# Seven quarter products in the MLP's up projection: one pair of units at a time

## The chip, the cores and the metric

The kernel runs on one core of one Trainium2 chip. The metric is the device time of one execution in microseconds. Five engines work from their own instruction streams: TensorE (PE, matmuls), VectorE (DVE), ScalarE (ACT), GpSimd (POOL) and SyncE (SP, which issues nearly all DMAs here). Matmul results go to PSUM, eight banks of 512 float32 values per partition. Everything else lies in SBUF.

## The reference, cut to what matters

Two layers of a hybrid decoder block for one sequence of 512 tokens with model width 1024, all in float32. Each layer has two mixing branches (a gated delta rule and a sliding-window attention), merged and projected, and then an MLP, which is what the change touches:

```python
h2 = rmsnorm(x, pre_mlp_g)                              # (512, 1024)
ff = jnp.square(jax.nn.relu(h2 @ w_ff1)) @ w_ff2        # 1024 -> 4096 -> 1024
x = x + rmsnorm(ff, post_mlp_g)
```

## The kernel before, in words

**Precision.** A float32 product is made of three matmuls of the rounded type float32r. Each operand is split into a high part (an ACT cast) and a low part (a DVE subtraction), and hi·hi, hi·lo and lo·hi are added in PSUM. So every weight chunk costs a load (SP), a cast `wh` (ACT, L323) and a subtraction `wl` (DVE, L324), all in `prefetch`.

**Weights.** `specs` lists all chunks in the order in which they are used. A chunk is 128 x 1024 values. `weights()` hands out the next one and calls `prefetch`, which prepares chunks up to three ahead of it: `LOOK` = 4 buffers each of `wh` and `wl`, and `WR` = 5 raw buffers `wr` that the loads fill. A `wh` buffer is free again after the last matmul that reads it.

**The MLP.** The 4096 hidden columns are four blocks s = 0 to 3 of 1024. A block has eight *units* of 128 hidden columns. One unit of the up product `h2 @ w_ff1` is `mm_a`: one weight chunk, eight slices of the contraction, three matmuls each, 512 tokens wide, into one bank of the pool "pm" (two banks). ACT then takes relu and square.

In blocks 0 to 2 the down product is done by a Strassen-Winograd scheme with seven products P1 to P7 instead of eight. `lefts` (L1345 on) makes the sums and splits of the activations for four units at once, `seven` makes the sums of weight quarters on DVE (`add`, L293), and `mm_c` (L400 to L404) multiplies: two chunks of 12 matmuls per product. The products stand in the order P1, P5, P6, P4, P7, P2, P3 and are added into `acc` by DVE. Block 3 is plain: eight units, then `mm_b4` for the first 512 output columns and `mm_b` or `last_tiles` for the others.

**Banks.** The tags are "pm" (2 banks, `PM`), "ps" (3, `PS`), "pk" (1, `PK`) and "ss" (2, `PZ`).

**Order.** A scheduler decides the order of instructions on each engine when the program is built, from priorities and its own estimate of times; on the chip each engine then runs its list in that fixed order. Where the source opens an `Order`, the instructions of the named engines keep the order of the source. A new tile takes a slot of its tag that has been released, and waits for one if there is none. `X4` is a tag of six 128 x 1024 tiles that raw activations, gains and residual rows share; `T[i]` are tags of four 128 x 512 tiles.

Of the kernel before, what the change touches and what calls it, by code (L numbers as in the profile page):

```python
# [49 lines left out]
PMB = 2  # L50


def chunk_order(depth):


    out = []
    for l in range(depth):
        a_in = lambda w, c: out.append(("chunk", w, l, 0, c, 0))
        b_in = lambda w, r, c, n: out.append(("chunk", w, l, r, c, n))
        for n in range(3):  # L60
            for j in range(4):
                b_in("w_in", j * 256, OFF_B + n * NB, NB)
        n_ = {"K": 0, "G": 0, "A": 0}
        for c in "".join(MIX):
            a_in("w_in", {"K": OFF_K, "G": OFF_GB, "A": OFF_GA}[c] + n_[c] * P)
            n_[c] += 1
        for h in range(H):
            for o in (OFF_V, OFF_Q, OFF_Z):
                a_in("w_in", o + h * P)
            if h == 0:  # L70
                for m in range(KT):
                    a_in("w_up_sw", m * P)
                for m in range(NA, NA2):
                    a_in("w_in", OFF_GA + m * P)
        for m in range(NA2, KT):
            a_in("w_in", OFF_GA + m * P)
        for m in range(KT):
            a_in("w_up_dn", m * P)
        for n in range(2):
            for j in range(4):  # L80
                b_in("w_o", j * 256, n * 512, 512)
        for s in range(4):
            for m in FF_ORDER if s < 3 else range(8):
                a_in("w_ff1", (s * 8 + m) * P)
            if s < 3:
# [34 lines left out]
def hybrid_trunk(ctx, tc, x, positions, pre_mix_g, dn_conv_w, dn_a_log, dn_dt_bias, dn_norm_g,  # L120
# [26 lines left out]
        return sm.tile([P, n], F32, name=name, bufs=1)  # L147

    US = pool_of("s", 8)
    T = [pool_of(f"t{i}", 4) for i in range(8)]  # L150

    def UQ(name, dt=F32):

# [37 lines left out]
    def c4(ap):  # L191
        return ap.rearrange("p (c i) -> p c i", c=4)
# [77 lines left out]
    def load(key):  # L270
# [3 lines left out]
        dma(wr[:, :w], wpk[index[key], :, :w])  # L274
        return wr

    def blocks(a, n_):
        return a[:, :2 * n_ if n_ else 1024].rearrange("p (k c) -> p k c", k=2 if n_ else 8)

    def seven(w, l, r0):  # L280

# [10 lines left out]
        def add(i, k, j):  # L292
# [22 lines left out]
    def prefetch(n, wr=None, sub=tt):  # L315
        while len(pre) < min(n, len(specs)):
# [5 lines left out]
            w = 2 * n_ if n_ else 1024  # L322
            nc.scalar.copy(wh[:, :w], wr[:, :w])  # L323
            sub(out=wl[:, :w], in0=wr[:, :w], in1=wh[:, :w].bitcast(F32), op=ALU.subtract)  # L324
            pre.append((blocks(wh, n_), blocks(wl, n_)))
# [65 lines left out]
    def mm_c(pss, left, onto=False):  # L391

        for j in range(2):
            wh, wl = weights()
            hi, lo = left[j]
            for t in range(2):
                for r in range(2):
# [6 lines left out]
                    mm(pss[t], lhsT=lo[:, c], rhs=wh[:, r, :], start=False, stop=last,  # L404
                       skip_group_check=onto)
# [34 lines left out]
    def root(xt):  # L440
        return rstd("nr", meansq(xt[:, :512], "nq0"), meansq(xt[:, 512:], "nq1"))

    def norm_half(xt, gb, r, g):

        xs = T[7]("xs")
# [21 lines left out]
        for g in range(2):  # L467
            turned(pss[g], t, qs[g])

    def post_tiles(tiles, a0g, ps1, add1, q0, gb, xsrc, xdst, gb2=None):  # L470


        n = range(len(tiles))
        rows = [slice(t * P, (t + 1) * P) for t in tiles]
        xt = [[T[5 + i]("xt") for i in range(2)] for t in tiles]
        for i in n:
            for k in range(2):
                dma(xt[i][k], xsrc[rows[i], k * 512:(k + 1) * 512])
# [19 lines left out]
        if gb2 is not None:  # L498
            q = [(meansq(xo[i][:, :512], "nq0"), meansq(xo[i][:, 512:], "nq1")) for i in n]
            for i in n:  # L500
                r = rstd("nr", *q[i])
                xs.append([norm_half(xo[i], gb2, r, g) for g in range(2)])
        order.end()
        return xs

# [14 lines left out]
    for l in range(depth):  # L520
# [816 lines left out]

        def ff2_tail(tiles, pss):
            a0, a1 = [a[0] for a in acc], [a[1] for a in acc]
            if l == depth - 1:  # L1340
                post_tiles(tiles, a0, pss, a1, s0, gb3, xd, give)
            else:
                xs_next.extend(post_tiles(tiles, a0, pss, a1, s0, gb3, xd, keep, nxt[0]))

        def lefts(X, Y):  # L1345

            a11, a21, a12, a22 = X[:, 0:512], X[:, 512:1024], Y[:, 0:512], Y[:, 512:1024]
            S = {n_: T[4](n_) for n_ in ("S1", "S2", "S3", "S4")}
            tt(out=S["S1"], in0=a21, in1=a22, op=ALU.subtract)
            tt(out=S["S2"], in0=a11, in1=S["S1"], op=ALU.subtract)  # L1350
            for name, U, src in (("P1", T[5], a11), ("P5", T[7], S["S1"]), ("P6", T[1], S["S2"]),
                                 ("P4", T[2], a22), ("P7", T[3], S["S3"]), ("P2", T[6], a12),
                                 ("P3", T[0], S["S4"])):
                if name == "P4":
                    tt(out=S["S4"], in0=a12, in1=S["S2"], op=ALU.subtract)
                    tt(out=S["S3"], in0=a21, in1=a11, op=ALU.subtract)
                p_ = pair(U, name)
                split(src, *p_)
                left[name].append(p_)

        for s in range(3):
            left = {f"P{i}": [] for i in range(1, 8)}
            raw = [None, None]
            for i, m in enumerate(FF_ORDER):
                if s == 0 and i < 4:
                    ps = early[i][0]
                else:
                    ps = PM("ps_f1")
                    mm_a(ps, h2)

                if i % 4 < 2:
                    raw[i % 2] = X4("raw")
                r_ = raw[i % 2].rearrange("p (a k n) -> p a k n", a=2, k=2)[:, :, m % 2, :]
                act(out=r_, in_=ps.rearrange("p (a n) -> p a n", a=2), func=AF.Relu)
                act(out=r_, in_=r_, func=AF.Square)
                if i % 4 == 3:
# [3 lines left out]
            v_ = [T[4]("p1") for t in range(2)]  # L1380
            for t in range(2):
                nc.scalar.copy(v_[t], pa[t])
            mm_c(pb_, left["P5"])
            for t in range(2):
                into(2 + t, 1, pb_[t])
            pc = [PS("ps_p6"), PK("ps_p6")]
            mm_c(pc, left["P6"])
            for t in range(2):
                tt(out=v_[t], in0=pc[t], in1=v_[t], op=ALU.subtract)
# [1 line left out]
                    nc.scalar.copy(acc[t][1], v_[t])  # L1391
                else:
                    tt(out=acc[t][1], in0=acc[t][1], in1=v_[t], op=ALU.add)
            pc = [PM("ps_p4"), PM("ps_p4")]
            mm_c(pc, left["P4"])
            for t in range(2):
                into(2 + t, 0, pc[t])
            pc = [PS("ps_p7"), PK("ps_p7")]
            mm_c(pc, left["P7"])
            for t in range(2):  # L1400
                tt(out=v_[t], in0=pc[t], in1=v_[t], op=ALU.add)
                for n, op in ((0, ALU.subtract), (1, ALU.add)):
                    tt(out=acc[2 + t][n], in0=acc[2 + t][n], in1=v_[t], op=op)
            mm_c(pa, left["P2"], True)
            for t in range(2):
                into(t, 0, pa[t])
            mm_c(pb_, left["P3"], True)
            for t in range(2):
                tt(out=acc[t][1], in0=pb_[t], in1=acc[t][1], op=ALU.add)


        gb3 = gain(post_mlp_g[l])
        h3 = []
        for m in range(8):
            ps = PM("ps_f1")
            mm_a(ps, h2)
            r_ = T[4]("relu")
            act(out=r_, in_=ps, func=AF.Relu)
            act(out=r_, in_=r_, func=AF.Square)
            p_ = pair(T[m % 4], "h3")  # L1420
            split(r_, *p_)
            h3.append(p_)
        pss = four(1)
        mm_b4(pss, h3)
        for t in range(NT):
# [40 lines left out]
```

## Time and profile before

| | |
|---|---|
| Median of three runs | 1830.43 us (1829.82 to 1830.57) |
| Span of the profiled execution | 1828.6 us |
| Time of the profiled execution itself | not listed; the median lies 1.8 us above its span |
| PE busy | 1809.1 us (99%) |
| Weight loads (PEld) busy | 1503.9 us (82%) |
| DVE busy | 1292.1 us (71%) |
| ACT busy | 940.9 us (51%) |
| POOL busy | 211.2 us (12%) |
| HBM read | 239.38 MB |

PE's busy time counts each matmul from its start to a modelled end, and consecutive matmuls overlap. So the rate is read from the distance between starts. Busy shares are averages over the whole span; the MLP's stages are read from a view that cuts the span into stretches. Rows of a group give its line, engine, operation, output and inputs, shapes and count, then busy time, mean length, and the engine's idle time before them with what ended it.

### The profile page before, as it was taken

What the parts mean: (1) busy time and instruction counts of PE and PEld (TensorE: products, weight loads), DVE (VectorE), ACT (ScalarE), POOL (GpSimd) and SP (SyncE); (2) the same over time, 40 slices, a digit from 0 to 9 for tenths busy, and PEclk for the clock granted to TensorE, in tenths of its full rate; (3) what the DMA queues carried; (4) which work ended last, traced back from release to release, by engine and by line L of the source; (5) the groups of instructions that cost most, each with busy time, mean ns of one, the idle gap of its engine ahead of it and who ended that gap; (6) DMA issues with size and microseconds to landing.
All of it is one profiled execution on the core that took longest, in us unless ns stands there. A gap on an engine that the chain in (4) does not pass through costs nothing.

```text
span 1828.6 us, 26748 instructions
## 1 busy us (share of the span) xinstructions
PE 1809.1 (99%) x9598; PEld 1503.9 (82%) x9598; DVE 1292.1 (71%) x2466; ACT 940.9 (51%) x1913; POOL 211.2 (12%) x386
## 2 busy tenths in 40 slices
PE   9999999999999999999999999999999999999998
PEld 8888778888788888888898887888887898888886
DVE  5499796887566758684556997968885568585934
ACT  6678742444434645544347877234444346554442
POOL 0322102221101000000003221022111010000000
PEclk9999999999999999999999999999999999999999
DMA  5633447554453363564245343485545534544631
GB/s 188 202 118 116 115 149 223 179 170 149 124 191 124 96 216 120 168 217 151 93 151 181 104 127 110 167 234 165 160 139 153 172 119 135 174 163 148 233 102 46
DMA packets 146422, 278.48 MB, mean 152 GB/s; under 512 B 33569, under 2 KB 66657, under 8 KB 146290
## 3 DMA queue, kind: packets, MB, share of 16 engines
q1 hardware_dynamic: 145778, 276.75, 47.4%
q8 instruction: 75, 1.23, 0.3%
q14 instruction: 57, 0.47, 0.1%
q0 software_dynamic: 512, 0.03, 0.0%
HBM read 239.38 MB, written 37.36 MB: 151 GB/s over the span
## 4 chain that ended last, share of the span: by engine, by line
PE 84%; DVE 6%; ACT 5%; DMA 3%; issue 1%; POOL 1%; SPq 0%; POOLq 0%; DVEq 0%; ACTq 0%
PE ps_f L340 6%; PE ps_f L339 6%; PE ps_f L341 6%; PE ps_p L402 3%; PE ps_p L404 3%; PE ps_p L400 3%; PE ps_b L388 3%; PE ps_b L387 3%; PE ps_b L389 3%; PE ps_vp L339 2%; PE ps_us L339 2%; PE ps_ud L339 2%; PE ps_vp L341 2%; PE ps_ud L341 2%; PE ps_ud L340 2%; PE ps_us L340 2%
## 5 line engine op out<-in xcount | busy, mean ns | idle before, releaser
L323 ACT CAST wh<-wr 128x1024 fp32r<-128x1024 f32 (+1 forms) x332 | 343.1, 1040 | 542.2 <-PE ps_f L340 145.8
L324 DVE TENSOR_TENSOR wl<-wr,wh 128x1024 fp32r<-128x1024 f32 (+1 forms) x332 | 400.4, 1216 | 303.6 <-ACT wh L323 300.6
L339 PE MATMUL ps_f<-g_h,wh 128*128 128x512 f32 x448 | 174.3, 389 | 0.0
L340 PE MATMUL ps_f<-g_l,wh 128*128 128x512 f32 x448 | 174.3, 389 | 0.0
L341 PE MATMUL ps_f<-g_h,wl 128*128 128x512 f32 x448 | 174.3, 389 | 0.0
L402 PE MATMUL ps_p<-wl,P_h 128*128 128x512 f32 x336 | 131.4, 391 | 0.4 <-DVE wl L324 0.3
L404 PE MATMUL ps_p<-wh,P_l 128*128 128x512 f32 x336 | 130.8, 389 | 0.0
L400 PE MATMUL ps_p<-wh,P_h 128*128 128x512 f32 x336 | 129.5, 389 | 0.0
L437 POOL TENSOR_TENSOR pr<-pq,pw 128x1 f32<-128x1 f32 x16 | 9.8, 613 | 807.6 <-DVE pq L436 807.6
L339 PEld LDWEIGHTS ps_f<-g_h,wh 128*128 128x128 f32 x448 | 84.1, 188 | 17.4
L341 PEld LDWEIGHTS ps_f<-g_h,wl 128*128 128x128 f32 x448 | 84.1, 188 | 17.4
L340 PEld LDWEIGHTS ps_f<-g_l,wh 128*128 128x128 f32 x448 | 84.1, 188 | 17.4
L402 PEld LDWEIGHTS ps_p<-wl,P_h 128*128 128x128 f32 x336 | 63.1, 188 | 15.8 <-DVE wl L324 2.4
L400 PEld LDWEIGHTS ps_p<-wh,P_h 128*128 128x128 f32 x336 | 63.1, 188 | 13.3
L404 PEld LDWEIGHTS ps_p<-wh,P_l 128*128 128x128 f32 x336 | 63.1, 188 | 12.8
L387 PE MATMUL ps_b<-wh,h_h 128*128 128x432 f32 (+1 forms) x192 | 71.1, 370 | 0.0
L388 PE MATMUL ps_b<-wl,h_h 128*128 128x432 f32 (+1 forms) x192 | 70.5, 367 | 0.3 <-DVE wl L324 0.3
L389 PE MATMUL ps_b<-wh,h_l 128*128 128x432 f32 (+1 forms) x192 | 70.2, 366 | 0.0
L293 DVE TENSOR_TENSOR wr<-wr 128x1024 f32<-128x1024 f32 x48 | 58.0, 1220 | 2.6 <-DMA wr<-in_weights_dram 1.9
L340 PE MATMUL ps_qp<-h_l,wh 128*128 128x512 f32 x128 | 54.0, 422 | 0.0
L339 PE MATMUL ps_vp<-h_h,wh 128*128 128x512 f32 x128 | 53.9, 421 | 0.0
L341 PE MATMUL ps_vp<-h_h,wl 128*128 128x512 f32 x128 | 53.6, 419 | 0.0
(359 smaller groups left out, 4873.6 us busy)
## 6 DMA issues: line engine op xcount, KB each, us to landing
wr<-in_weights_dram SPq DMA_DIRECT2D x320, 512.0 KB, 3.5
wr<-in_weights_dram SPq DMA_DIRECT2D x24, 432.0 KB, 3.6
D<-dd SPq DMA_DIRECT2D x32, 256.0 KB, 3.2
xd<-xo SPq DMA_DIRECT2D x12, 512.0 KB, 2.8
xt<-xd SPq DMA_DIRECT2D x24, 256.0 KB, 3.7
D<-gd SPq DMA_DIRECT2D x16, 256.0 KB, 6.5
dd<-D SPq DMA_DIRECT2D x16, 256.0 KB, 3.9
kkd<-kk SPq DMA_DIRECT2D x16, 256.0 KB, 2.0
```

Source lines behind the costliest of these rows:

```text
L293: tt(out=held[j], in0=held[j], in1=part(i, k, j), op=ALU.add)
L323: nc.scalar.copy(wh[:, :w], wr[:, :w])
L324: sub(out=wl[:, :w], in0=wr[:, :w], in1=wh[:, :w].bitcast(F32), op=ALU.subtract)
L339: mm(ps, lhsT=wh[:, k, :], rhs=hi, start=k == 0, stop=False)
L340: mm(ps, lhsT=wh[:, k, :], rhs=lo, start=False, stop=False)
L341: mm(ps, lhsT=wl[:, k, :], rhs=hi, start=False, stop=k == KT - 1)
L387: mm(pss[t], lhsT=hi[:, tsl], rhs=wh[:, r, :], start=k == 0, stop=False)
L388: mm(pss[t], lhsT=hi[:, tsl], rhs=wl[:, r, :], start=False, stop=False)
L389: mm(pss[t], lhsT=lo[:, tsl], rhs=wh[:, r, :], start=False, stop=k == KT - 1)
L400: mm(pss[t], lhsT=hi[:, c], rhs=wh[:, r, :], start=first, stop=False, skip_group_check=onto)
L402: mm(pss[t], lhsT=hi[:, c], rhs=wl[:, r, :], start=False, stop=False, skip_group_check=onto)
L404: mm(pss[t], lhsT=lo[:, c], rhs=wh[:, r, :], start=False, stop=last, skip_group_check=onto)
```

## The change

**Pairs of units.** Two units m and m+1 of an up block are now computed together as a product of 2 x 2 quarters: the 512 tokens are halved (256 each), and so are the contraction (4 slices each). The two units are the other cut of the output. Seven products of quarters take the place of eight. Each is `mm_h`: 4 slices, 3 matmuls each, 256 tokens wide. Block 3 is four such pairs; block 2 has two pairs amid four single units; blocks 0 and 1 keep single units.

- The weights of a pair are two loaded chunks `0` and `1`, two chunks `a` and `b` of sums made by four DVE additions of 128 x 512, and the second half of `1` alone: three and a half chunks to cast and to subtract instead of two. `WR` becomes 6.
- The activations need four combinations n1 to n4 (of 1024 x 256 values each), made once per layer by `combos` during block 1 and kept in `T[0]`, `T[3]`, `T[6]` and the new `T[8]` until block 3 is done.
- Partial sums stay in PSUM. Each role has its bank: a in "pm", y in "ss", z in "ps", q in "pk". ACT copies a to y and y to z between banks, and PE adds the next product onto the copy. PE's order inside these blocks is that of the source, and the last two products of a pair come after the first one of the next.

**Down products.** The order becomes P1, P5, P6, P2, P4, P7, P3. The splits for P2, P7 and P3 are made later, after P1, P5 and P6, into the tiles that these leave. P6 and P7 use the "pm" banks, P4 uses "ps" and "pk".

**Others.** The tail's residual tiles use `T[0]`, `T[3]`, `T[6]`; the descriptor space of POOL's DMAs is set to 4096.

```diff
-WR = 5
+WR = 6
+SEQ = (FF_ORDER, FF_ORDER, (0, 1, (4, 5), (2, 3), 6, 7), ((0, 1), (2, 3), (4, 5), (6, 7)))
...
                  lambda j: add(1, 1, j),
+                 lambda j: part(1, 0, j),
                  lambda j: add(1, 0, j),
                  lambda j: (take(0, 1, j), add(1, 1, j))[1],
-                 lambda j: part(1, 0, j),
                  lambda j: part(1, 1, j))
...
+    def up_specs(l, s):
...
+            def sums():
+                if "a" not in b:
+                    for n_ in ("a", "b"):
+                        b[n_] = wp.tile([P, 1024], F32, name="wr", bufs=WR)
...
+                    for o_, i0, i1 in ((ya, x0, x2), (yb, ya, x3), (yd, x2, x3), (yc, yb, x1)):
+                        tt(out=o_, in0=i0, in1=i1, op=ALU.add)
...
+            out.append((raw if two else lambda m=e: unit(m), 0))
+            if last:
+                out.append((last, -1))
+            last = None
+            if two:
+                out += [(fb, 0), (fa, 0)] if n == 0 else [(fa, 0), (fb, 0)]
+                last = tail
...
+    def mm_h(ps, w, k0, op, start):
+
+        wh, wl = w
+        for k in range(4):
+            hi, lo = op[k]
+            mm(ps, lhsT=wh[:, k0 + k, :], rhs=hi, start=start and k == 0, stop=False,
+               skip_group_check=True)
+            mm(ps, lhsT=wh[:, k0 + k, :], rhs=lo, start=False, stop=False, skip_group_check=True)
+            mm(ps, lhsT=wl[:, k0 + k, :], rhs=hi, start=False, stop=k == 3, skip_group_check=True)
...
+        def combos():
...
+            a21, n1 = whole(0, 1), whole(1, 1)
+            tt(out=n1, in0=n1, in1=a21, op=ALU.subtract)
+            to("n1", n1, T[0])
+            yield
+            a11 = whole(0, 0)
+            tt(out=n1, in0=a11, in1=n1, op=ALU.add)
+            to("n2", n1, T[3], -1.0)
+            tt(out=a21, in0=a11, in1=a21, op=ALU.subtract)
+            to("n3", a21, T[6])
+            yield
+            a12 = whole(1, 0)
+            tt(out=a12, in0=n1, in1=a12, op=ALU.subtract)
+            yield
+            to("n4", a12, T[8])
+
+        def ff1(done):
+            order = Order(nc.tensor)
+            order.begin()
+            rest = lambda: None
+            for n, e in enumerate(SEQ[s]):
+                if not isinstance(e, tuple):
+                    ps = PM("ps_f1")
+                    w = weights()
+                    mm_a(ps, h2, range(4), w)
+                    rest()
+
+                    def rest(ps=ps, w=w, e=e):
+                        mm_a(ps, h2, range(4, 8), w)
+                        done((e,), ps)
+                    continue
+
+                R = X4("raw")
+                a, y, z, q = PM("ps_a"), PZ("ps_y"), PS("ps_z"), PK("ps_q")
+                a, y, z, q = (b[:, half(0)] for b in (a, y, z, q))
+                q_ = R[:, half(2)]
+                c1 = weights()
+                mm_h(a, c1, 0, ops["a11"], True)
+                nc.scalar.copy(y, a)
+                rest()
+
+                def seventh():
+                    c = weights()
+                    mm_h(q, c, 4, ops["n3"], True)
+                    nc.scalar.copy(q_, q)
+                    return c
+
+                if n == 0:
+                    c3 = seventh()
+                c2 = weights()
+                mm_h(y, c2, 4, ops["n2"], False)
+                nc.scalar.copy(z, y)
+                mm_h(a, c1, 4, ops["a12"], False)
+                act(out=R[:, half(0)], in_=a, func=AF.Relu)
+                if n > 0:
+                    c3 = seventh()
+                mm_h(z, c2, 0, ops["n1"], False)
+                stt(out=R[:, half(3)], in0=z, scalar=-1.0, in1=q_, op0=ALU.mult, op1=ALU.subtract)
+
+                def rest(e=e, R=R, y=y, z=z, q_=q_, c3=c3):
+                    mm_h(y, c3, 0, ops["a22"], False)
+                    tt(out=R[:, half(2)], in0=y, in1=q_, op=ALU.add)
+                    act(out=R[:, 512:], in_=R[:, 512:], func=AF.Relu)
+                    mm_h(z, weights(), 0, ops["n4"], False)
+                    act(out=R[:, half(1)], in_=z, func=AF.Relu, scale=-1.0)
+                    act(out=R, in_=R, func=AF.Square)
+                    done(e, R)
+            rest()
+            order.end()
...
+            make_later("P2", T[5])
             mm_c(pb_, left["P5"])
...
-            pc = [PS("ps_p6"), PK("ps_p6")]
+            make_later("P7", T[7])
+            pc = [PM("ps_p6"), PM("ps_p6")]
             mm_c(pc, left["P6"])
...
-            pc = [PM("ps_p4"), PM("ps_p4")]
+            make_later("P3", T[1])
+            mm_c(pa, left["P2"], True)
+            for t in range(2):
+                into(t, 0, pa[t])
+            pc = [PS("ps_p4"), PK("ps_p4")]
             mm_c(pc, left["P4"])
...
-            pc = [PS("ps_p7"), PK("ps_p7")]
+            pc = [PM("ps_p7"), PM("ps_p7")]
             mm_c(pc, left["P7"])
...
-        for m in range(8):
-            ps = PM("ps_f1")
-            mm_a(ps, h2)
...
+        ff1(done)
         pss = four(1)
```

More of the change, by code (lines that the diff above doesn't have):

```diff
@@ L50, with units @@
 PMB = 2
+def units(seq):
+    return [m for e in seq for m in (e if isinstance(e, tuple) else (e,))]
 def chunk_order(depth):
@@ L82, in chunk_order @@
         for s in range(4):
-            for m in FF_ORDER if s < 3 else range(8):
-                a_in("w_ff1", (s * 8 + m) * P)
+            out.append(("up", l, s))
             if s < 3:
@@ L99, in chunk_keys @@
             keys[tuple(key)] = None
+        elif kind == "up":
+            l, s = key
+            for m in units(SEQ[s]):
+                keys["w_ff1", l, 0, (s * 8 + m) * P, 0] = None
         else:
@@ L149, in hybrid_trunk @@
     US = pool_of("s", 8)
-    T = [pool_of(f"t{i}", 4) for i in range(8)]
+    T = [pool_of(f"t{i}", 4) for i in range(9)]
     def UQ(name, dt=F32):
@@ L501, in post_tiles @@
                 r = rstd("nr", *q[i])
-                xs.append([norm_half(xo[i], gb2, r, g) for g in range(2)])
+                xs.append([norm_half(xo[i], gb2, r, g, Tx[2]) for g in range(2)])
         order.end()
@@ L1339, in ff2_tail @@
             a0, a1 = [a[0] for a in acc], [a[1] for a in acc]
+            Tx = T[0], T[3], T[6]
             if l == depth - 1:
-                post_tiles(tiles, a0, pss, a1, s0, gb3, xd, give)
+                post_tiles(tiles, a0, pss, a1, s0, gb3, xd, give, None, Tx)
             else:
[L1343 to L1357, printed above, removed]
+                xs_next.extend(post_tiles(tiles, a0, pss, a1, s0, gb3, xd, keep, nxt[0], Tx))
@@ new lines, in hybrid_trunk, with whole, to @@
+        half = lambda i: slice(i * 256, (i + 1) * 256)
+        hb = lambda g, i: [tuple(a[:, half(i)] for a in h2[g * 4 + k]) for k in range(4)]
+        ops = {"a11": hb(0, 0), "a12": hb(1, 0), "a22": hb(1, 1)}
+        def combos():
+            def whole(g, i):
+                a = X4("hs")
+                hi, lo = (c4(x_)[:, :, half(i)] for x_ in q2[g])
+                tt(out=c4(a), in0=hi.bitcast(F32), in1=lo.bitcast(F32), op=ALU.add)
+                return a
+            def to(name, src, T_, sign=1.0):
+                ts_ = [(T_(name + "_h", F32R), T_(name + "_l", F32R)) for i in range(2)]
+                for i, (hi, lo) in enumerate(ts_):
+                    x_ = src[:, i * 512:(i + 1) * 512]
+                    if sign > 0:
+                        split(x_, hi, lo)
+                        continue
+                    act(out=hi, in_=x_, func=AF.Copy, scale=-1.0)
+                    stt(out=lo, in0=x_, scalar=-1.0, in1=hi.bitcast(F32), op0=ALU.mult,
+                        op1=ALU.subtract)
+                ops[name] = [tuple(a[:, half(k % 2)] for a in ts_[k // 2]) for k in range(4)]
+            a21, n1 = whole(0, 1), whole(1, 1)
[12 more added lines that the diff above has]
+            to("n4", a12, T[8])
@@ L1409, in hybrid_trunk, with done @@
                 tt(out=acc[t][1], in0=pb_[t], in1=acc[t][1], op=ALU.add)
+            if s == 1:
+                next(cg, None)
+        s = 3
         gb3 = gain(post_mlp_g[l])
-        h3 = []
-        for m in range(8):
[L1415 to L1422, printed above, removed]
+        h3 = [None] * 8
+        def done(ms, R):
+            for i, m in enumerate(ms):
+                h3[m] = pair(T[(1, 2, 5, 7)[m % 4]], "h3")
+                split(R.rearrange("p (a k n) -> p a k n", a=2, k=2)[:, :, i, :],
+                      *(a.rearrange("p (a n) -> p a n", a=2) for a in h3[m]))
+        ff1(done)
         pss = four(1)
```

104 lines of the change are left out of this document (81 added, 23 removed).

## The prediction

> **What bounds the kernel now.** I read the page's busy times and its chain of waits first:
>
> ```profile
> span 1828.6 us, 26748 instructions
> ...
> PE 1809.1 (99%) x9598; PEld 1503.9 (82%) x9598; DVE 1292.1 (71%) x2466; ACT 940.9 (51%) x1913; POOL 211.2 (12%) x386
> ...
> PE 84%; DVE 6%; ACT 5%; DMA 3%; issue 1%; POOL 1%; SPq 0%; POOLq 0%; DVEq 0%; ACTq 0%
> ...
> xt<-xd SPq DMA_DIRECT2D x24, 256.0 KB, 3.7
> ```
>
> TensorE (PE) is busy nearly all the span. The change sits in the MLP, so I then cut layer 0's MLP into stages (columns: length, then each engine's busy time, clock, DMA share): up block 1, its down products, up block 2, its down products, up block 3, the first half of the last down.
>
> ```profile
> 664.10:707.70 43.60, 43.60 (x195) 36.08 (x194) 21.73 (x25) 20.81 (x31) 0.00 (x0) 1.00 0.34 107
> 707.70:745.80 38.10, 37.91 (x167) 31.01 (x166) 36.83 (x45) 19.62 (x24) 0.00 (x0) 1.00 0.58 195
> 745.80:789.20 43.40, 43.40 (x193) 35.95 (x192) 22.47 (x26) 20.77 (x30) 0.00 (x0) 1.00 0.43 144
> 789.20:827.40 38.20, 38.05 (x168) 31.12 (x167) 36.39 (x45) 19.67 (x24) 0.00 (x0) 1.00 0.69 235
> 827.40:871.00 43.60, 43.60 (x194) 36.09 (x193) 16.88 (x18) 20.66 (x29) 0.00 (x0) 1.00 0.40 138
> 871.00:897.00 26.00, 26.00 (x116) 21.53 (x115) 11.64 (x14) 9.59 (x16) 0.00 (x0) 1.00 0.24 76
> ```
>
> Up blocks: PE full at clock 1.00, DVE half idle. Down products: PE full, DVE full too. So time falls only if PE's own time falls, and DVE has room in one kind of stage, none in the other.
>
> A matmul's printed length overlaps the next one's; its real price is the distance between starts. Two stretches of PE's timeline, 512 columns and 256 columns wide:
>
> ```profile
> 606.07 0.39 PE L339 MATMUL ps_f<-g_h,wh 128*128 128x512 f32 x1
> ...
> 608.79 0.39 PE L339 MATMUL ps_f<-g_h,wh 128*128 128x512 f32 x1
> ```
>
> ```profile
> 590.09 0.28 PE L351 MATMUL ps_f<-g_l,wh 128*128 128x256 f32 x1
> ...
> 603.89 0.28 PE L352 MATMUL ps_f<-g_h,wl 128*128 128x256 f32 x1
> ```
>
> The first pair is 12 matmuls apart: 2.72/12 = 0.2267 us. The second is 115 apart: 13.80/115 = 0.1200 us. Half the columns cost 53%, not 50%.
>
> **The change, part by part.**
>
> *PE's products.* A pair of units was 2 x 24 = 48 matmuls of 512 columns, 48 x 0.2267 = 10.88 us. It becomes seven groups of 12 with 256 columns, 84 x 0.1200 = 10.08 us. Gain 0.80 us, not the eighth (1.36) that the arithmetic saves. Six pairs in each of two layers: 12 x 0.80 = **9.6 us off**. The 256-wide row above is the same kind of instruction (same operands, a slice of the same bank), so I take it unchanged.
>
> The Trainium skill, "TensorE: Matmul & The Clock Gate", section "Back-to-back issue gap", gives for a lone stream columns/2.4 ns plus 2.5 ns. By that, 512 columns would cost 215.8 and 256 would cost 109.2, and the pairs would give 12 x (48 x 215.8 - 84 x 109.2) ns = 14.2 us (an estimate from that page). The rows say 226.7 and 120.0: about 13 ns above columns/2.4 at both widths, so narrowing is dearer here than the rule has it. The measurement decides.
>
> *Engines beside the pairs.* Groups of DVE and ACT in the MLP, and the 256-wide relatives elsewhere (min/median/max ns):
>
> ```profile
> L324 DVE TENSOR_TENSOR wl<-wr,wh 128x1024 fp32r<-128x1024 f32 x57 | 68.6, 1220 | 80.3 <-ACT wh L323 80.3
> L293 DVE TENSOR_TENSOR wr<-wr 128x1024 f32<-128x1024 f32 x16 | 19.3, 1218 | 0.5 <-DMA wr<-in_weights_dram 0.4
> L412 DVE TENSOR_TENSOR P_l<-S,P_h 128x512 fp32r<-128x512 f32 x16 | 10.8, 683 | 0.0
> L1349 DVE TENSOR_TENSOR S<-raw 128x512 f32<-128x512 f32 x4 | 2.8, 692 | 0.0
> ```
>
> ```profile
> L323 ACT CAST wh<-wr 128x1024 fp32r<-128x1024 f32 x57 | 59.5, 1053 | 116.2 <-PE ps_f L340 64.9 <-PE ps_p L404 22.1 <-DVE wr L293 15.7
> L411 ACT CAST P_h<-S 128x512 fp32r<-128x512 f32 x16 | 9.7, 619 | 1.8 <-DVE S L1355 1.2 <-DVE S L1350 0.6
> L1374 ACT ACTIVATE raw<-ps_f 128x512 f32<-128x512 f32 x16 | 9.5, 592 | 0.0
> ```
>
> ```profile
> L899 ACT COPY M<-ps_s x48: 361/373/385, 116.7 to 1133.0; 128x256 f32<-128x256 f32 x48
> ```
>
> ```profile
> L896 DVE TENSOR_TENSOR M<-ps_s,ban x16: 414/418/425, 81.5 to 1011.7; 128x256 f32<-128x256 f32 x16
> ```
>
> Back to back, DVE starts come closer than these lengths. Its timeline in the third down stage:
>
> ```profile
> 790.83 1.23 DVE L324 TENSOR_TENSOR wl<-wr,wh 128x1024 fp32r<-128x1024 f32 x1 [2.35 <-ACT wh L323]
> ...
> 799.21 2.35 DVE L293 TENSOR_TENSOR wr<-wr 128x1024 f32<-128x1024 f32 x2
> 801.48 0.68 DVE L1332 TENSOR_TENSOR acc<-ps_p,acc 128x512 f32<-128x512 f32 x1
> ...
> 820.31 2.49 DVE L1403 TENSOR_TENSOR acc<-acc,p 128x512 f32<-128x512 f32 x4
> 822.72 2.35 DVE L324 TENSOR_TENSOR wl<-wr,wh 128x1024 fp32r<-128x1024 f32 x2
> ...
> 829.65 1.21 DVE L324 TENSOR_TENSOR wl<-wr,wh 128x1024 fp32r<-128x1024 f32 x1
> ```
>
> 2.27/2 = 1.135 us for 1024 columns, 2.41/4 = 0.60 for 512. A pair in the last block then asks of DVE: low parts of three and a half units 3 x 1.135 + 0.60, four weight sums 2.40, two 256-wide sums at 0.42, two splits 1.20: 8.45 us of 10.08. ACT: casts 3 x 1.05 + 0.62; three 256-wide copies and two 256-wide relus at 0.373; relu 0.62, square 1.05, two casts 1.24: 8.5 of 10.08. Both fit.
>
> Does each hand-over fit? A group of twelve lasts 1.44 us. The order is a11, then the previous pair's last two groups, n2, a12, n3, n1. The copy a to y has two groups (2.88 us) for 0.37; y to z likewise; the subtraction that frees z has two. A summed chunk's buffer comes free after n1 and is wanted three groups (4.32 us) later; cast and low part need 1.05 + 1.22 = 2.27. I take **0** per pair. ACT's and DVE's other work hides behind those two to three groups; if that cover is gone, a 1.05 us cast ahead of a copy costs about that much. PSUM-to-PSUM copies have no row: below by nothing (hidden), above by the 512-wide 0.592.
>
> *Single to pair in the third block.* Singles 0 and 1 hold both "pm" banks, and their halves go 0, 1, 0; then the first pair's a11 wants a "pm" bank. It waits for the relu of single 0, with no PE work between. What is due on ACT just then is shown by the end of a chunk in the last block, first PE, then ACT:
>
> ```profile
> 833.54 0.39 PE L341 MATMUL ps_f<-g_h,wl 128*128 128x512 f32 x1
> 833.77 0.39 PE L339 MATMUL ps_f<-g_h,wh 128*128 128x512 f32 x1
> ```
>
> ```profile
> 833.74 1.05 ACT L323 CAST wh<-wr 128x1024 fp32r<-128x1024 f32 x1 [4.16 <-PE ps_f L340]
> 834.69 0.59 ACT L1418 ACTIVATE relu<-ps_f 128x512 f32<-128x512 f32 x1
> ```
>
> The cast waits for the very buffer that this chunk frees, goes first, and the relu ends at 835.28, 1.5 us after the next start was due. In the third block the cast of the pair's second sum stands the same way. With the hand-over I take **1.6 us a layer, 3.2 in all**; bounds: 0.7 if the relu goes first, 2.6 if a second cast is ahead. Behind the waiting a11 stand all later matmuls.
>
> *Third down stage into the last block.* DVE worked without a real gap from 790.83 to 830.86 (40 us) beside 38.2 of PE. The change adds: three of six postponed splits come in from the up block, 1.8 us; the sums of pair 0, 2.4. That is 44.2. Of it 3.6 can slip past the block's start (four sums of P7, two of P3). 40.6 must be done before pair 0's third chunk is used, 2.9 us into the block; DVE has about 38.2 + 2.9 less the first cast's 1.05, 40.0. I take **0.6 us a layer, 1.2 in all**, between 0 and 2.5. After that DVE gains 1.6 us a pair and catches up.
>
> *Down products reordered.* PE's present waits there:
>
> ```profile
> 726.73 0.39 PE L400 MATMUL ps_p<-wh,P_h 128*128 128x512 f32 x1
> 727.31 0.50 PE L402 MATMUL ps_p<-wl,P_h 128*128 128x512 f32 x1 [0.19 <-DVE wl L324]
> ```
>
> ```profile
> 809.35 0.50 PE L402 MATMUL ps_p<-wl,P_h 128*128 128x512 f32 x1 [0.15 <-DVE wl L324]
> ```
>
> ```profile
> 806.34 1.22 DVE L293 TENSOR_TENSOR wr<-wr 128x1024 f32<-128x1024 f32 x1 [0.18 <-DMA wr<-in_weights_dram]
> ```
>
> Both are the second chunk of the fourth product, whose weight sum waited for a load. That place gets P2, a plain part without a sum, and the raw pool a sixth buffer. The first starts 0.35 late (due 0.2267 after 726.73) and the matmul is 0.11 longer than the usual 0.39: 0.46. These two and, taken alike, layer 1's two make 1.8. I count **-0.8**, nearly half, since P4's sum moves one product on and DVE is fuller; bounds -1.8 to +1.8.
>
> *Activation sums* in the second up block: eight 1024-wide and eight 512-wide DVE operations, 9.1 + 4.8 = 13.9 us, ACT eight casts 5.0. That stage has 43.4 - 22.5 = 21 us of DVE and 22 of ACT free: **0**; without that cover up to 13.9 a layer.
>
> *The rest:* no load is added, only the order on SP's queue changes. P6 and P7 get the "pm" banks; P7's are freed by DVE with P3's 24 matmuls (5.44 us) still to run. The residual's tiles can now load only after the last pair, 26 us before use (last window) for 3.7 us: **0**. The smaller descriptor space touches POOL's few issues, all outside the MLP.
>
> **Sum:** -9.6 + 3.2 + 1.2 - 0.8 = -6.0. The profiled execution has no time of its own in what is shown; its span 1828.6 lies 1.8 under the median 1830.43. Its span goes to 1822.6, the time to **1824.4**. A measurement here can tell about 0.2% (3.7 us) from no change.
>
> **Rivals.**
>
> *A, everything hides.* No new wait, the present ones gone: -9.6 - 1.8, 1819.0. For: half-idle DVE in up blocks. Against: the bank wait, forced by two banks. 0.15.
>
> *B, DVE becomes the bound.* In the third down stage and the last block DVE is asked 44.2 + 4 x 8.45 = 78.0 us beside 38.2 + 40.3 = 78.5 of PE. If it also idles for ACT between cast and low part, nothing is left over: 2.5 us at each start instead of 0.6, and 0.3 in each of the eight pairs: 3.8 + 2.4 more, 1830.6, no change. For: the full DVE window. Against: those two splits and P7's sums can wait. 0.19.
>
> *C, ACT's order puts PE in line: slower.* ACT takes its work in a fixed order. The casts wait at its head for weight buffers, as the row above shows (64.9 us on ps_f alone). If a copy that PE accumulates onto stands behind such a cast and the square, PE waits about 1.05 + 1.05 + 0.37 - 1.44 = 1.0 us past the group that covers it; at one such place a pair, 12 x 1.0 more: 1836.4. It decides from 0.5 us a pair (6.0 us over twelve), where the gain is gone. For: the cast-before-relu pair above. Against: the copies have two groups, not one. 0.14. The Trainium skill, same page, its table of specifications, calls ScalarE's queue strictly first-in first-out, eight deep; the two ACT rows agree with the order, though not with a depth.
>
> *D, the weight loads show.* Loads per pair rise from 48 to 84. If each cost its own length instead of hiding under a 256-column matmul, 84 x 0.19 = 16.0 us a pair, 12 x 5.9 over the taken price: about 1895. Its length stands here:
>
> ```profile
> 590.21 0.19 PEld L350 LDWEIGHTS ps_f<-g_h,wh 128*128 128x128 f32 x1
> 590.33 0.19 PEld L351 LDWEIGHTS ps_f<-g_l,wh 128*128 128x128 f32 x1
> ```
>
> Against: loads start 0.12 apart, at the matmuls' pace. 0.02.
>
> *E, the 256-wide matmuls run nearer to columns/2.4* (0.109 against 0.216): 14.2 off instead of 9.6, 1819.8. The 115 steps at 0.120 speak against it. 0.03; the rule is the page's above.
>
> **How the numbers follow.** Forecast 0.47, with its own range 1822 to 1828 (bank wait 0.7 to 2.6 a layer, start 0 to 1.5, down stages). A 0.15, B 0.19, C 0.14, D 0.02, E 0.03. Range 1819 to 1834: D, most of C and the edge of A stay out. Faster: 0.45 of the forecast, A, E and 0.03 of B: 0.66. Same: most of B and a little of the forecast: 0.16. Slower: C, D, the rest: 0.18.
>
> **What would show it.** 84 matmuls a pair 0.120 apart; one PE wait of 1.5 us on a relu some 8 us into the third up block; a short wait on DVE's low part early in the last block; none inside pairs; the fourth product's wait gone. Wrong would be: repeated PE waits on ACT copies (C) or on low parts in every pair (B), or 256-wide starts further apart than 0.120.

## The result and the profile after

The changed kernel takes 1835.25 us (median of 11 runs, 1833.34 to 1837.04); the kernel before, run beside it, 1830.57 (11 runs, 1829.82 to 1832.2). The ratio is 1.0025, with a 95% interval of 1.0017 to 1.0033. So the change made the kernel slower, by 4.7 us, where 6.0 us less was forecast. The profiled execution took 1836.3 us, its span 1834.6, which is 6.0 above the span before.

First the page of the changed kernel: the span, the busy times and the shares of the chain of waits by engine.

```profile
span 1834.6 us, 27883 instructions
...
PE 1805.6 (98%) x10030; PEld 1521.4 (83%) x10030; DVE 1377.9 (75%) x2594; ACT 975.4 (53%) x1989; POOL 211.8 (12%) x386
...
PE 81%; DVE 10%; ACT 4%; issue 2%; DMA 1%; POOL 1%; SPq 0%; DVEq 0%; POOLq 0%; ACTq 0%
```

TensorE's busy time fell by only 3.5 us, and VectorE (DVE) now holds 10% of the chain instead of 6%. Layer 0's MLP, cut at the first matmul of each stage, shows where. The columns are those of the prediction's table of stages; the rows are the second up block (s = 1, the prediction's "up block 1"), its down products, the third up block (s = 2), its down products, the last up block (s = 3), and the first half of the last down products.

```profile
664.67:708.19 43.52, 43.52 (x193) 36.05 (x192) 33.70 (x39) 23.17 (x36) 0.00 (x0) 1.00 0.36 110
708.19:746.89 38.70, 38.48 (x169) 31.38 (x168) 37.64 (x47) 21.18 (x27) 0.00 (x0) 1.00 0.52 176
746.89:790.59 43.70, 42.25 (x266) 38.09 (x265) 31.15 (x40) 23.78 (x38) 0.00 (x0) 1.00 0.44 133
790.59:829.29 38.70, 38.48 (x169) 31.37 (x168) 38.46 (x49) 19.06 (x25) 0.00 (x0) 1.00 0.52 177
829.29:875.50 46.21, 43.44 (x338) 43.01 (x336) 35.52 (x50) 30.30 (x50) 0.00 (x0) 0.93 0.43 139
875.50:897.28 21.78, 21.78 (x98) 18.03 (x97) 9.89 (x12) 8.52 (x14) 0.00 (x0) 1.00 0.67 218
```

The kernel before, cut the same way, has 43.52 us for every one of these up blocks; its last one reads:

```profile
828.33:871.85 43.52, 43.52 (x194) 36.04 (x192) 15.95 (x18) 20.70 (x30) 0.00 (x0) 1.00 0.39 135
```

| stage | before, layer 0 / 1 | after, layer 0 / 1 | forecast, a layer |
|---|---|---|---|
| second up block | 43.52 / 43.52 | 43.52 / 43.52 | 0 |
| third up block (two pairs, one bank wait) | 43.52 / 43.52 | 43.70 / 43.69 | -1.6 + 1.6 = 0 |
| last up block (four pairs) | 43.52 / 43.52 | 46.21 / 46.01 | -3.2 + 0.6 = -2.6 |
| the three down stages (s = 0 to 2) | 115.50 / 115.02 | 115.48 / 115.52 | -0.4 |

The differences are +2.85 us in layer 0 and +3.16 in layer 1: the 6.0 of the spans. One row carries the miss. The last up block was to last about 40.9 us and took 46.2, and it is the only one whose granted clock (0.93) isn't 1.00.

Inside that block TensorE's timeline shows two waits, and then slow steps (start, length, and in brackets the idle time with what ended it):

```profile
830.60 0.28 PE L472 MATMUL ps_a<-g_h,wl 128*128 128x256 f32 x1
832.91 0.38 PE L469 MATMUL ps_q<-n_h,wh 128*128 128x256 f32 x1 [2.03 <-ACT wh L380]
...
834.17 0.58 PE L472 MATMUL ps_q<-n_h,wl 128*128 128x256 f32 x1 [0.74 <-DVE wl L381]
...
835.19 0.41 PE L469 MATMUL ps_q<-n_h,wh 128*128 128x256 f32 x1
835.40 0.41 PE L471 MATMUL ps_q<-n_l,wh 128*128 128x256 f32 x1
```

After the first pair's a11 TensorE has nothing until 832.91: the product n3 needs the cast of a weight sum, and then the sum's low part. From 835.19 to 835.40 one step is 0.21 us instead of 0.12. From about 840 it is 0.12 again, and every further group of twelve lasts 1.44 us, as forecast. Stretches of the same block give the granted clock (third column from the right):

```profile
828.00:830.60 2.60, 2.60 (x18) 2.37 (x17) 2.60 (x6) 0.00 (x0) 0.00 (x0) 1.00 0.01 5
...
835.00:837.50 2.50, 2.50 (x13) 2.50 (x13) 2.50 (x4) 0.37 (x1) 0.00 (x0) 0.50 0.46 123
837.50:840.00 2.50, 2.50 (x14) 2.50 (x13) 1.38 (x3) 0.36 (x1) 0.00 (x0) 0.50 0.23 93
840.00:842.00 2.00, 2.00 (x18) 2.00 (x18) 0.29 (x1) 0.91 (x2) 0.00 (x0) 0.98 0.71 254
```

So two costs lie in the first pair. The waits with their restarts cost some 3.4 us of the 5.9 that this block is above 40.32 us (four pairs at 10.08). The rest, 2.5, is a clock of 0.50 for some 7 us afterwards. The Trainium skill, "TensorE: Matmul & The Clock Gate", section "What's actually happening", names a cold state at half the clock; a step of 0.21 us for 256 columns agrees with its 1.2 GHz (256/1.2 = 213 ns).

Why the sum is late stands in VectorE's timeline:

```profile
825.03 1.28 DVE L1597 TENSOR_TENSOR p<-ps_p,p 128x512 f32<-128x512 f32 x2
826.23 2.49 DVE L1599 TENSOR_TENSOR acc<-acc,p 128x512 f32<-128x512 f32 x4
828.63 1.89 DVE L339 TENSOR_TENSOR wr<-wr 128x512 f32<-128x512 f32 x3
830.44 0.68 DVE L1602 TENSOR_TENSOR acc<-ps_p,acc 128x512 f32<-128x512 f32 x1
831.04 0.68 DVE L339 TENSOR_TENSOR wr<-wr 128x512 f32<-128x512 f32 x1
```

VectorE's order was fixed when the program was built. Ahead of the pair's four weight sums (L339) stand the six sums of P7 (L1597, L1599), and ahead of the fourth a sum of P3 (L1602). That is seven sums of 0.60 us, 4.2 us in all. P3's sum needs TensorE's last product of the down stage, but that product did not hold VectorE up: TensorE was in the next block from 829.29, and VectorE shows no idle time before 830.44. What makes the fourth weight sum late is the length of the work ahead of it. It is over at about 831.7; the cast (1.05 us) follows, and then n3.

### The profile page after: what moved, and what is told of

Same layout as the page of the kernel before. It is cut to its first block, busy times and chain, and to the rows that moved or that the text cites. A ratio compares the mean times of both kernels' runs of the same rounds, so it can differ in the third digit from the quotient of the medians.

```text
span 1834.6 us, 27883 instructions
## 1 busy us (share of the span) xinstructions
PE 1805.6 (98%) x10030; PEld 1521.4 (83%) x10030; DVE 1377.9 (75%) x2594; ACT 975.4 (53%) x1989; POOL 211.8 (12%) x386
## 3 DMA queue, kind: packets, MB, share of 16 engines
q8 instruction: 79, 1.29, 0.3%
## 4 chain that ended last, share of the span: by engine, by line
PE 81%; DVE 10%; ACT 4%; issue 2%; DMA 1%; POOL 1%; SPq 0%; DVEq 0%; POOLq 0%; ACTq 0%
PE ps_f L397 3%; PE ps_f L396 3%; PE ps_f L398 3%; PE ps_b L444 3%; PE ps_b L445 3%; PE ps_b L446 3%; DVE wl L381 2%; PE ps_p L459 2%; PE ps_p L461 2%; PE ps_p L457 2%; PE ps_vp L396 2%; PE ps_vp L398 2%; PE ps_vp L397 2%; PE ps_us L396 2%; PE ps_ud L396 2%
## 5 line engine op out<-in xcount | busy, mean ns | idle before, releaser
L380 ACT CAST wh<-wr 128x1024 fp32r<-128x1024 f32 (+2 forms) x356 | 361.9, 1026 | 477.4 <-PE ps_f L397 69.8
L381 DVE TENSOR_TENSOR wl<-wr,wh 128x1024 fp32r<-128x1024 f32 (+2 forms) x356 | 422.2, 1197 | 217.1 <-ACT wh L380 213.9
L396 PE MATMUL ps_f<-g_h,wh 128*128 128x512 f32 x256 | 99.7, 389 | 0.0
L397 PE MATMUL ps_f<-g_l,wh 128*128 128x512 f32 x256 | 99.7, 389 | 0.0
L398 PE MATMUL ps_f<-g_h,wl 128*128 128x512 f32 x256 | 99.6, 389 | 0.0
L398 PEld LDWEIGHTS ps_f<-g_h,wl 128*128 128x128 f32 x256 | 48.1, 188 | 10.1
L396 PEld LDWEIGHTS ps_f<-g_h,wh 128*128 128x128 f32 x256 | 48.1, 188 | 9.8
L397 PEld LDWEIGHTS ps_f<-g_l,wh 128*128 128x128 f32 x256 | 48.1, 188 | 9.6
```

The costliest lines, as they stand in the source:

```text
L396: mm(ps, lhsT=wh[:, k, :], rhs=hi, start=k == 0, stop=False)
L397: mm(ps, lhsT=wh[:, k, :], rhs=lo, start=False, stop=False)
L398: mm(ps, lhsT=wl[:, k, :], rhs=hi, start=False, stop=k == KT - 1)
```

## The experiments

### One look-ahead earlier: e1

The four weight sums of the last block's first pair are put in the order as soon as its two units have been asked for, ahead of P7's and P3's sums. By the list of chunks that is one chunk earlier, not two as the expectation below has it. Nothing is taken away.

```
-        def one(ms):
+        def one(ms, soon):
             def raw():
                 b["0"], b["1"] = (unit(m) for m in ms)
+                if soon:
+                    sums()
                 return b["0"]
...
-                raw, fa, fb, tail = one(e)
+                raw, fa, fb, tail = one(e, s == 3 and n == 0)
```

> The changed kernel, but the four weight sums of the last block's first pair are asked for with the pair's first chunk, two chunks earlier than before, so that on VectorE they stand ahead of the third down product's last sums. Theory 'place in the order': in the changed kernel the fourth sum stands behind a sum that waits for TensorE itself, so the first pair loses 5.9 us a layer against 1.44 us a group; here the first pair's five groups last 7.2 us instead of 13.1, the clock stays at 1.00, and the time is about 1835.3 - 2 x 5.5 = 1824. Rival 'too much work': VectorE is simply full there; then the wait moves into the third down stage (38.7 us becomes 41 or more) or stays, and the time is within 3 us of 1835.

Measured: 1827.9 us (11 runs, 1825.71 to 1829.35); the kernel before beside it 1829.95; ratio 0.9988 (0.9979 to 0.9997). The same amount of work in another order is some 7 us below the changed kernel. One row of TensorE's timeline, and the last block:

```profile
832.91 0.39 PE L474 MATMUL ps_q<-n_h,wl 128*128 128x256 f32 x1 [1.19 <-DVE wl L383]
```

```profile
829.88:871.65 41.77, 40.58 (x337) 40.36 (x336) 35.22 (x50) 28.58 (x49) 0.00 (x0) 1.00 0.48 153
```

The wait for the cast is gone, the wait for the low part is longer (1.19 instead of 0.74), and the clock stays at 1.00. The down stage ahead keeps its 38.70 us. The place in the order sets the loss, not the amount of work. It is not all: 1.2 us a layer remain, and the 1824 of the expectation was not reached. The expectation's theory holds for the order, and not for its reason: P3's sum had its operand in time, as the timeline of VectorE above shows.

### The single's bank: e2

The order of the third up block becomes single, pair, single, pair, so that a pair's a11 no longer asks for the bank of a single whose relu is still due.

```
-SEQ = (FF_ORDER, FF_ORDER, (0, 1, (4, 5), (2, 3), 6, 7), ((0, 1), (2, 3), (4, 5), (6, 7)))
+SEQ = (FF_ORDER, FF_ORDER, (0, (4, 5), 1, (2, 3), 6, 7), ((0, 1), (2, 3), (4, 5), (6, 7)))
```

> The changed kernel with the third block's order 0, pair 4-5, 1, pair 2-3, 6, 7 instead of 0, 1, pair, pair, 6, 7, so that a pair's 'pm' bank was never just filled. Theory 'bank wait': the 1.45 us wait on ScalarE's relu before the first pair goes, the third up block falls from 43.7 to 42.1 us, and the time by 3.2 us to about 1832. Rival: two 'pm' banks are short anyway, the wait comes back at another pair or single, and the time stays within 1 us of 1835.

In the changed kernel, the timelines of TensorE and of ACT at that place are:

```profile
754.83 0.39 PE L398 MATMUL ps_f<-g_h,wl 128*128 128x512 f32 x1
756.66 0.38 PE L469 MATMUL ps_a<-g_h,wh 128*128 128x256 f32 x1 [1.45 <-ACT raw L1549]
```

```profile
755.07 1.04 ACT L380 CAST wh<-wr 128x1024 fp32r<-128x1024 f32 x1 [2.31 <-PE ps_f L397]
756.02 0.59 ACT L1549 ACTIVATE raw<-ps_f 128x512 f32<-128x512 f32 x1
```

The cast goes first, the relu ends at 756.61, and the a11 starts at 756.66 instead of 755.06: 1.60 us late. With the other order, the same block and then two stretches after the wait in the last block:

```profile
746.49:788.51 42.02, 42.02 (x265) 38.16 (x264) 30.94 (x40) 24.75 (x39) 0.00 (x0) 1.00 0.43 138
...
834.00:836.00 2.00, 2.00 (x11) 2.00 (x11) 2.00 (x4) 0.37 (x1) 0.00 (x0) 0.50 0.66 229
836.00:840.00 4.00, 4.00 (x35) 4.00 (x34) 1.92 (x4) 1.93 (x4) 0.00 (x0) 0.99 0.38 147
```

The third up block falls by 1.68 us to 42.02, with no wait left, and the last block keeps its wait (1.98) and its half clock. The time is 1830.43 us (11 runs, 1827.9 to 1832.06), ratio 1.0000 (0.9991 to 1.0008): 4.8 below the changed kernel for 3.4 taken out of the stages. Part of the other 1.4 can be that the half clock does not last equally long every time. Here it ended at about 836 in layer 0 and the last block took 45.06 us; in layer 1, with the same two waits, it lasted twice as long and the block took 46.19. Over the eleven executions the mean granted clock was 0.996 to 0.999 here and 0.995 to 0.998 in the changed kernel. How much of the 1.4 this makes was not separated.

### The clock by itself: e3

Ahead of n3, eighteen transposes keep TensorE at work while it would wait. Their result is not used, so they are added work, and the wait for the weight sum stays.

```
                 if n == 0:
+                    for _ in range(18):
+                        tr(qq_[:, 256:384], ident, ident)
                     c3 = seventh()
```

(qq_ is the whole bank of which q is the half in use.)

> The changed kernel with 18 transposes of the identity (128 wide, about 0.07 us each, into an unused part of a bank) between the first two groups of the last block, where TensorE sits idle for 2.0 us; they compute nothing that is used. Theory 'clock': the wait for the weights stays (next group starts at the same time), but TensorE isn't idle for long, the granted clock stays 1.00 instead of 0.50 for some 6.8 us, and 2.5 us a layer come back: about 1830. Rival 'the slow matmuls come from elsewhere' (low parts or banks that arrive late): the 0.213 us steps stay and the time is within 1 us of 1835.

TensorE's timeline, then a stretch just behind it:

```profile
830.23 2.13 PE L1489 MATMUL ps_q<-ident 128*128 128x128 f32 x18
832.42 0.39 PE L469 MATMUL ps_q<-n_h,wh 128*128 128x256 f32 x1
...
833.67 0.39 PE L472 MATMUL ps_q<-n_h,wl 128*128 128x256 f32 x1 [0.76 <-DVE wl L381]
```

```profile
835.00:837.50 2.50, 2.50 (x24) 2.50 (x23) 2.50 (x4) 0.73 (x2) 0.00 (x0) 1.00 0.64 200
```

The product n3 starts 2.19 us after a11's last group is over, as in the changed kernel (830.72 to 832.91 there), and the wait for the low part is the same (0.76). But the clock stays at 1.00, and in 2.50 us there are 24 matmuls where the changed kernel had 13. The last up block takes 43.62 and 43.59 us: 2.6 and 2.4 below the changed kernel. So the idle time itself brings the half clock, and this is some 2.5 us of each layer's 5.9. The time shows less of it: 1832.72 us (11 runs, 1831.72 to 1834.13), 2.5 below the changed kernel, ratio 1.0013 (1.0004 to 1.0022) to the kernel before, where about 1830 was expected. In the profiled execution some of it is lost to longer waits in the attention, which this edit does not touch: TensorE is idle 3.3 us between 1100 and 1500 us, in the changed kernel 1.5. Whether that is chance was not tried. Besides, the changed kernel's profiled execution has the lowest mean clock of its eleven (0.995, the others 0.996 to 0.998; e3 has 0.999 in all), so in its median the half clock cost less than in the profile.

### Both orders, and the last sums: e4 and e6

e4 takes the edits of e1 and e2 together.

> Both edits, early sums and the third block's order 0, pair, 1, pair, 6, 7. If both theories hold the gains add: 1835.3 - 11 - 3.2 = about 1821, some 9.5 us below the kernel before, which is the 12 x 0.80 us that the narrower products save. If VectorE's load is the limit: 1830 or above.

Measured: 1823.38 us (5 runs, 1822.89 to 1824.85), ratio 0.9964 (0.9951 to 0.9976), some 2.4 above the 1821 of the expectation. One wait is left in the pairs of each layer. VectorE and TensorE:

```profile
826.91 2.48 DVE L1601 TENSOR_TENSOR acc<-acc,p 128x512 f32<-128x512 f32 x4
829.32 2.35 DVE L383 TENSOR_TENSOR wl<-wr,wh 128x1024 fp32r<-128x1024 f32 x2
```

```profile
830.59 0.38 PE L474 MATMUL ps_q<-n_h,wl 128*128 128x256 f32 x1 [1.17 <-DVE wl L383]
```

Four sums of P7 that nobody waits for stand ahead of two low parts that TensorE waits for. e6 adds to e4 that these four come after P3's product in the order:

```
             for t in range(2):
                 tt(out=v_[t], in0=pc[t], in1=v_[t], op=ALU.add)
+            mm_c(pb_, left["P3"], True)
+            for t in range(2):
                 for n, op in ((0, ALU.subtract), (1, ALU.add)):
                     tt(out=acc[2 + t][n], in0=acc[2 + t][n], in1=v_[t], op=op)
-            mm_c(pb_, left["P3"], True)
```

> The kernel with early sums and the order 0, pair, 1, pair, 6, 7, and besides P7's four sums into the accumulators written after P3's matmuls, so that on VectorE they stand behind the low parts that the last block's first pair needs. With early sums and the new order that pair still waited 1.17 us for a low part that stood behind those four sums (2.4 us). Theory 'place in the order': that wait goes, 2 x 1.35 us, about 1820.7. Rival 'VectorE is full': the low part is late anyway, or the two sums of P3 are late and hold banks; the time stays at 1823.

Measured: 1821.82 us (5 runs, 1821.33 to 1822.67) beside 1830.34, ratio 0.9952 (0.9939 to 0.9966). This version beats both kernels, the one before by 8.5 us, and lies 1.1 above the 1820.7 of the expectation. Its VectorE at that place, and its third and last up blocks:

```profile
825.91 2.36 DVE L383 TENSOR_TENSOR wl<-wr,wh 128x1024 fp32r<-128x1024 f32 x2
828.19 2.49 DVE L1603 TENSOR_TENSOR acc<-acc,p 128x512 f32<-128x512 f32 x4
```

```profile
745.75:787.77 42.02, 42.02 (x265) 38.16 (x264) 31.13 (x40) 24.85 (x39) 0.00 (x0) 1.00 0.47 138
...
826.48:867.01 40.53, 40.53 (x338) 40.36 (x336) 35.14 (x50) 28.59 (x49) 0.00 (x0) 1.00 0.49 156
```

Now the same two instruction groups stand the other way round, TensorE is busy for all of both up blocks, and the last one takes 40.53 us. VectorE had the time all along.

### The sums on another engine: e5

e4 with all the pairs' weight sums on GpSimd, which does nothing in the MLP.

```
-                        tt(out=o_, in0=i0, in1=i1, op=ALU.add)
+                        ptt(out=o_, in0=i0, in1=i1, op=ALU.add)
```

> The kernel with early sums and the order 0, pair, 1, pair, 6, 7, but with all four weight sums of every pair on GpSimd instead of VectorE (1.28 us each by a 128x512 product there, against 0.60 on VectorE; 5.1 us of GpSimd a pair of 10.1). It takes 2.4 us off VectorE a pair. If VectorE's load sets the first pair's remaining wait (1.17 us): it shrinks to some 0.3, about 1821.5. If the longer sums themselves are late (5.1 us instead of 2.4 before the casts): waits inside pairs or at the first pair, 1824 or more.

Measured: 1836.8 us (5 runs, 1833.93 to 1838.23), ratio 1.0033 (1.002 to 1.0045): 13.4 above e4. Its groups of GpSimd (POOL), then the timelines of VectorE and of GpSimd:

```profile
L341 POOL TENSOR_TENSOR wr<-wr 128x512 f32<-128x512 f32 x48 | 88.7, 1866 | 460.2 <-DMA wr<-in_weights_dram 333.6 <-DVE wl L383 63.6 <-ACT wh L382 62.0
L1177 POOL TENSOR_TENSOR qe<-qq,egb 128x512 f32<-128x512 f32 x16 | 20.5, 1280 | 34.2 <-DVE qq L787 26.3 <-PE ps_i L1084 7.0
```

```profile
818.60 5.73 DVE L383 TENSOR_TENSOR wl<-wr,wh 128x1024 fp32r<-128x1024 f32 x4
...
825.45 5.76 DVE L1601 TENSOR_TENSOR acc<-acc,p 128x512 f32<-128x512 f32 x4
```

```profile
820.99 11.35 POOL L341 TENSOR_TENSOR wr<-wr 128x512 f32<-128x512 f32 x6 [61.24 <-DVE wl L383]
```

An addition takes 1.87 us on GpSimd here (mean of 48, the quickest 1.29), where a multiplication of the same shape in the attention takes 1.28. And VectorE, which was to be relieved, slows: its four 512-wide sums take 5.69 us from start to start of the next, where they took 2.41, and its four low parts 5.65 where they took 4.54. The first pair waits 1.13 and 2.86 us, and the last block takes 46.08 us; the third up block gets a wait of 0.80 us and takes 43.07. Some three GpSimd operations run in those 5.69 us; by the lone lengths, 2.41 + 3 x 1.28 = 6.3 us, they go nearly one behind the other. The Trainium skill, "SBUF — State Buffer", section "SBUF: two separate sides", says of these two engines that a VectorE operation with two SBUF inputs and a GpSimd operation hold a shared pair of ports in turn. The run agrees roughly: 5.69 is a little less than a strict turn would make of it.

### Pairs in the last block alone: e8

e6 with the third up block as single units, as before the change.

```
-SEQ = (FF_ORDER, FF_ORDER, (0, (4, 5), 1, (2, 3), 6, 7), ((0, 1), (2, 3), (4, 5), (6, 7)))
+SEQ = (FF_ORDER, FF_ORDER, FF_ORDER, ((0, 1), (2, 3), (4, 5), (6, 7)))
```

> As the kernel with early sums and P7's sums later, but the third up block in single units as before; only the last block has pairs. If each pair saves 0.80 us wherever it stands: four pairs a layer keep 6.4 us, so 3.2 us above the one with pairs in both blocks, about 1824. If pairs amid singles bring nothing (handovers between the two kinds): the same time as with pairs in both, 1821.

Measured: 1825.21 us (7 runs, 1824.24 to 1826.45), ratio 0.997 (0.996 to 0.9981). That is 3.4 above e6 for four pairs fewer, where the price of a pair gives 3.2. Its third up block takes 43.52 us and its last 40.53, in both layers. The 0.80 us a pair hold in both places.

### How long an idle time halves the clock: e7

The kernel before, with one idle time after each of the units 1 to 6 of its last up block: a transpose of a tile that ACT copies once to three times (wider for some units). The copies and the transposes are added work whose result is not used, and TensorE's order is fixed in that block.

```
+            if 1 <= m <= 6:
+                n_ = 512 if m % 2 == 0 else P
+                g_ = T[6]("gap")[:, 0:n_]
+                nc.scalar.copy(g_, ps[:, 0:n_])
+                for _ in range((m - 1) // 2):
+                    act(out=g_, in_=g_, func=AF.Copy, scale=1.0)
+                gp = PK("ps_gap")
+                tr(gp[:, 0:P], g_[:, 0:P], ident)
```

> The kernel before with six waits put into the last up block of each layer: after units 1 to 6 TensorE does one transpose that needs a chain of one to three copies on ScalarE that begins when the unit ends (nothing of it is used). Idle times of about 1.5, 1.8, 2.2, 3.0, 3.2 and 4 us, 5.4 us of full work between them. Theory 'clock follows idleness': idle times up to about 1.5 us are followed by matmuls at 0.227 us, idle times of 2 us and more by a stretch of some 6 us at half clock (0.44 us a matmul). Rival 'the slow stretch in the changed kernel belongs to its low parts and banks': all steps stay at 0.227.

TensorE's timeline after the third and after the fourth of the six:

```profile
855.27 0.33 PE L1426 MATMUL ps_gap<-ident,gap 128*128 128x128 f32 x1 [1.77 <-ACT gap L1424]
...
855.67 0.39 PE L340 MATMUL ps_f<-g_l,wh 128*128 128x512 f32 x1
855.90 0.40 PE L341 MATMUL ps_f<-g_h,wl 128*128 128x512 f32 x1
...
863.48 0.36 PE L1426 MATMUL ps_gap<-ident,gap 128*128 128x128 f32 x1 [2.41 <-ACT gap L1424]
...
864.07 0.63 PE L340 MATMUL ps_f<-g_l,wh 128*128 128x512 f32 x1
864.50 0.63 PE L341 MATMUL ps_f<-g_h,wl 128*128 128x512 f32 x1
...
867.05 0.41 PE L341 MATMUL ps_f<-g_h,wl 128*128 128x512 f32 x1
867.30 0.40 PE L339 MATMUL ps_f<-g_h,wh 128*128 128x512 f32 x1
```

After 1.77 us the next 512-wide steps are 0.23 us; after 2.41 they are 0.43 for some 3 us, and only at 867 near 0.23 again. Idle times of 1.07, 1.40 and 1.77 us left the clock alone, those of 2.41, 2.49 and 3.45 halved it for 3.4 us each (the expectation had some 6), and layer 1 shows the same six answers. The one run took 1869.14 us.

## Why the prediction was wrong

The step that failed is *Third down stage into last block*. It was put at 0.6 us a layer, at most 2.5, and measured 5.9 and 5.7. Two things in it were wrong.

- Its reasoning counted VectorE's work: 40.6 us asked of 40.0, after letting "four sums of P7, two of P3" slip past the block's start. Five of these six did not slip: in the changed kernel's order they stand ahead of the pair's fourth weight sum, 5 x 0.60 = 3.0 us that the balance had left out. The deadline was wrong too. The prediction wants the sums by "pair 0's third chunk", 2.9 us into the block; but in the first pair (`n == 0` in the diff) n3 comes right behind a11, and its weights are the chunk of the last two sums. So they are wanted 1.44 us into the block, where TensorE's wait of 2.03 us begins. e1 and e6 do the same work in another order and win the loss back, first some 7 us of the time, then in e6 all of the block but 0.2 us. The prediction should have written down the order of VectorE and of TensorE at this one place, as it did for ACT at the bank wait.
- It put the price of a late sum at the length of the wait. An idle time of 2.0 us also halved the clock for some 7 us. e3 separates it: about 2.5 of the 5.9 in the profiled execution.

The other steps, in their order:

- *PE's products*, -9.6: right. Groups of twelve last 1.44 us, and e8 against e6 prices four pairs at 3.4 us. The 0.120 us a step, read from another stage, carried over; what rival E asked for (0.109) did not appear.
- *Engines beside the pairs*, 0: right behind the first pair. The page of e6 has no wait left inside any pair. This also answers C (no copy put TensorE in line) and D (84 loads a pair hide).
- *Single to pair in the third block*, +1.6 a layer: right in size and in cause, 1.60 us late, a cast ahead of the relu. e2 removes it.
- *Down products reordered*, -0.8: wrong sign, +0.5, within its bounds. The waits of the fourth product for a low part are gone, but a new one stands in their place; the page of the changed kernel's waits of TensorE (us in total, times, the longest) has it, with the largest of the MLP above it:

```profile
PE ps_q L469 <- ACT wh L380: 4.0, 2, 2.0
...
PE ps_p L457 <- ACT wh L380: 0.9, 4, 0.2
```

  The last row is four times 0.22 us for a cast, once in the down stages of blocks 1 and 2 of each layer, and it is there in e6 too. What puts that cast behind was not tried.
- *Activation sums*, 0: right, the second up block is 43.52 us before and after with 33.70 us of VectorE's work in it.

Put together with what was measured: -9.6 for the pairs, +3.2 for the banks, +11.6 for the two starts, +0.5 for the down products is +5.7, beside 6.0 of the spans.

Of the rivals, C came nearest by its time (1836.4), which is luck: the waits that it is made of did not appear. B (1830.6) had the place, a late start of the last block at up to 2.5 us, though it named the wrong thing. It said that VectorE has no time left, and wanted 0.3 us in each of eight pairs, which none shows. In the changed kernel VectorE is busy 35.5 us of the last block's 46.2, and in e6 35.1 of 40.5 without making TensorE wait.

## What to carry to other kernels

Where an engine's order is fixed, list at the seam between two stages what stands ahead of the operation that the next stage waits for, with its length, and read from the next stage's own order when that operation is due: a balance of busy times can't show this. Put a new stage's first inputs ahead of the old stage's last sums, which nobody waits for. Where a wait of TensorE can reach 2 us, count the half clock behind it too, and before work is moved to an idle engine, count what the two take from each other.

## What was not expected of the hardware

- An idle time of 2.0 us (1.98 to 2.03) or more halved TensorE's clock, and 1.77 us or less did not, over twelve gaps in e7 and the first pairs here. By the trace's record of the clock the half clock lasted 3.41 us each of the six times in e7, and 6.83 us, twice that, in both layers of the changed kernel, where a second wait (0.74 and 0.46 us) falls into it. In layer 0 of e2 the second wait was over before the half clock began, and it lasted 3.41 us; but in e5 the end of a wait falls into it too, and it lasted 3.41 us all the same. What makes it one such stretch or two stays open, and so does whether one idle time decides or all the idle time within a stretch. The Trainium skill, "TensorE: Matmul & The Clock Gate", section "Why this matters for your kernels", asks for no idle gaps above some 3 us. Here 2 us sufficed, so the measurement decides; that its section "What's actually happening" puts the way back at a busy window of some 3.4 us agrees with e7.
- VectorE's 512-wide sums took 1.42 us each instead of 0.60 while GpSimd added beside them, and GpSimd 1.87 instead of 1.28 (e5).
